# Summing rows from contiguous 8 MiB blocks instead of from 112 rows per partition

## Chip, cores, metric

One core of one Trainium2 chip. The time is device microseconds of that core, the median of several executions, all with a granted clock of 1.0. A profile is one execution, and its span is some 1.8 us shorter than the time measured for the same execution.

## The reference

```python
batch, seq, dim = 32, 512, 1024
x = np.random.randn(batch, seq, dim).astype(np.float32)      # 67.1 MB
out = (np.sum(x, axis=-1) * 0.5).astype(np.float32)          # 16384 sums, 64 KiB
```

16384 rows of 4 KiB are read, and each gives one number.

## The kernel before

The rows are cut into eight blocks of 128 partitions x 16 rows (8 MiB). Three buffers hold blocks; VectorE (DVE) sums them, ScalarE (ACT) takes half of the seventh and about half of the eighth. The first seven blocks come from one region in which partition p owns 112 rows in a row; block b takes rows 16b to 16b+15 of each partition. So a load is 128 runs of 64 KiB that lie 448 KiB apart, and the 112 results of a partition leave as one run of 448 B. The last block is a region of its own, 16 rows to a partition, loaded in five pieces so that little work is left after the last byte.

```python
own = rows - B                                   # 128 - 16 = 112
x_rows = x_flat[0 : P * own, :].rearrange("(p c) d -> p c d", p=P)
x_last = x_flat[P * own : N, :].rearrange("(p c) d -> p c d", p=P)
out_rows = out_flat[0 : P * own].rearrange("(p c) -> p c", p=P)
out_last = out_flat[P * own : N].rearrange("(p c) -> p c", p=P)
# ... cut ...
for b in range(n_blocks - 1):
    c0 = b * B
    t = x_pool.tile([P, B, D], fp32, name="xb")
    loads.append(nc.sync.dma_start(out=t, in_=x_rows[:, c0 : c0 + B, :]))
    h = B if b < n_blocks - 2 else B // 2
    nc.vector.reduce_sum(out=sums[:, c0 : c0 + h], in_=t[:, 0:h, :], axis=mybir.AxisListType.X)
    # ... res = sums * mul on DVE; rows h..B on ACT
# ... last block: five loads of x_last, then
early = nc.sync.dma_start(out=out_rows, in_=res[:, 0:own])
# ... sums of the last block on DVE and ACT
store = nc.sync.dma_start(out=out_last, in_=res[:, own:])
# ... the program ends when early and store have landed
```

## Time and profile before

| | before |
|---|---|
| time, median (6 runs) | 162.07 us (161.97 to 162.15) |
| span of the profile | 160.2 us |
| DMA engines busy | 97.4% |
| a block's landing to the next one's | 19.35 us (433.5 GB/s) |
| first block in use | 21.78 us |
| last load to end of span | 157.5 to 160.2 us |

The DMA engines are the bound. VectorE waits 1.9 us for every block after the first, and the reduce starts work as a clock for landings (the moments at which all bytes of a transfer have arrived): when a load is slow, the next start comes late and the idle time in its square brackets grows.

### The profile page before, as it was taken

The numbers are of one execution on the slowest core, as the hardware profiler recorded it, in microseconds if no ns is written. First come the engines' busy times: TensorE is split into PE (matmuls) and PEld (weight loads), VectorE is DVE, ScalarE is ACT, GpSimd is POOL, SyncE is SP. The second block draws the span as 40 slices with busy tenths as digits, with TensorE's granted clock in tenths as the row PEclk, the third lists the DMA queues.
The fourth block names the chain that finished last, engine by engine and source line by source line (L and its number), as shares of the span: only waits on it lengthen the run. The fifth ranks groups of instructions, "written<-read, shape, count | busy, mean of one in ns | idle before, by whom it ended". The sixth has DMA issues, their size and how long they took to land.

```text
span 160.2 us, 138 instructions
## 1 busy us (share of the span) xinstructions
DVE 119.3 (74%) x34; ACT 17.3 (11%) x31; POOL 0.2 (0%) x4
## 2 busy tenths in 40 slices
DVE  0000059997799969999599995999959999597443
ACT  0000000000000000000000000000000000599952
POOL 0000000000000000000000000000000000000000
DMA  7996996996996996997997998979969969999992
GB/s 278 507 524 262 524 524 262 524 524 262 524 524 262 524 524 262 524 475 311 524 442 344 524 409 376 524 311 475 524 278 507 524 278 507 393 393 425 430 399 72
DMA packets 2016, 67.18 MB, mean 419 GB/s; under 512 B 480, under 2 KB 608, under 8 KB 736
## 3 DMA queue, kind: packets, MB, share of 16 engines
q1 hardware_dynamic: 2016, 67.18, 97.4%
HBM read 67.11 MB, written 0.07 MB: 419 GB/s over the span
## 4 chain that ended last, share of the span: by engine, by line
DMA 75%; DVE 22%; SPq 1%; issue 0%; DVEq 0%
DMA xb<-in_x_dram 75%; DVE sums L96 22%; SPq L114 1%; DVE xb L80 0%; SPq L120 0%; SPq L94 0%; DVE res L99 0%; DVEq L205 0%
## 5 line engine op out<-in xcount | busy, mean ns | idle before, releaser
L96 DVE TENSOR_REDUCE sums<-xb 128x16 f32<-128x16384 f32 (+1 forms) x7 | 112.0, 16001 | 33.3 <-DMA xb<-in_x_dram 33.3
L70 ACT ACT_TABLE_LOAD x1 | 1.3, 1283 | 137.9 <-DMA xb<-in_x_dram 137.9
L70 ACT ACTIVATE xb<-xb 128x1024 f32<-128x1024 f32 x15 | 15.7, 1045 | 2.1 <-DMA xb<-in_x_dram 2.1
L80 DVE CUSTOM_DVE_ANT_0 xb<-xb 128x512 f32<-128x512 f32 (+1 forms) x9 | 5.6, 664 | 5.0 <-DMA xb<-in_x_dram 5.0
L70 ACT ACTIVATION_READ_ACCUMULATOR xb<-xb 128x1 f32 x15 | 2.8, 187 | 0.0
L99 DVE TENSOR_SCALAR res<-sums 128x16 f32<-128x16 f32 (+1 forms) x7 | 1.2, 174 | 0.2
L80 DVE DVE_READ_ACCUMULATOR2_ANT res<- 128x1 f32 x9 | 0.7, 83 | 0.0
L80 DVE CUSTOM_DVE_ANT_0 xb<-xb,part 128x224 f32<-128x224 f32 x1 | 0.5, 450 | 0.2 <-DMA xb<-in_x_dram 0.2
L191 POOL MEMSET const-bfloat16-1.0<- 128x1 bf16 x1 | 0.1, 101 | 0.0
L191 POOL MEMSET const-uint8-127<- 128x1 uint8 x1 | 0.1, 101 | 0.0
L191 POOL MEMSET const-float32-0.0<- 128x1 f32 x1 | 0.1, 98 | 0.2 <-issue 0.2
L191 POOL MEMSET const-float32-1.0<- 128x1 f32 x1 | 0.1, 98 | 0.0
L80 DVE DVE_READ_ACCUMULATOR2_ANT part<- 128x1 f32 x1 | 0.1, 83 | 0.0
## 6 DMA issues: line engine op xcount, KB each, us to landing
xb<-in_x_dram SPq DMA_DIRECT2D x1, 4096.0 KB, 31.1
xb<-in_x_dram SPq DMA_DIRECT2D x1, 2560.0 KB, 36.9
xb<-in_x_dram SPq DMA_DIRECT2D x1, 1024.0 KB, 38.9
xb<-in_x_dram SPq DMA_DIRECT2D x1, 288.0 KB, 39.1
xb<-in_x_dram SPq DMA_DIRECT2D x1, 224.0 KB, 39.2
xb<-in_x_dram SPq DMA_DIRECT2D x7, 40.8
out_dram<-res SPq DMA_DIRECT2D x1, 56.0 KB, 10.0
out_dram<-res SPq DMA_DIRECT2D x1, 8.0 KB, 1.4
```

The source lines that it names most:

```text
L70: acts.append(nc.scalar.activation(out=t[:, r, :], in_=t[:, r, :], func=mybir.ActivationFunctionType.Copy, scale=mul, accum_out=res[:, col ...
L80: return nc.vector.tensor_tensor_reduce(out=t[:, r, lo:mid], in0=t[:, r, lo:mid], in1=t[:, r, mid:hi], scale=mul, scalar=start, op0=ADD, o ...
L96: nc.vector.reduce_sum(out=sums[:, c0 : c0 + h], in_=t[:, 0:h, :], axis=mybir.AxisListType.X)
L99: nc.vector.tensor_single_scalar(out=res[:, c0 : c0 + h], in_=sums[:, c0 : c0 + h], scalar=mul, op=mybir.AluOpType.mult,)
L114: nc.sync.dma_start(out=t[:, lo:hi, :], in_=x_last[:, lo:hi, :])
L191: nc = _bacc.Bacc("TRN2", target_bir_lowering=False, num_devices=1)
```

## The change

The intent: each load reads 8 MiB in one piece. Partition p's run starts 64p KiB into the block, so the pitch from partition to partition is 64 KiB instead of 448. The price is that a partition's results of seven blocks are no longer neighbours in the output: the first store becomes 7 x 128 rows of 64 B.

```diff
-    x_rows = x_flat[0 : P * own, :].rearrange("(p c) d -> p c d", p=P)
-    x_last = x_flat[P * own : N, :].rearrange("(p c) d -> p c d", p=P)
-    out_rows = out_flat[0 : P * own].rearrange("(p c) -> p c", p=P)
-    out_last = out_flat[P * own : N].rearrange("(p c) -> p c", p=P)
+    x_blocks = x_flat.rearrange("(b p c) d -> b p c d", p=P, c=B)
+    out_blocks = out_flat.rearrange("(b p c) -> p b c", p=P, c=B)
 ...
-        loads.append(nc.sync.dma_start(out=t, in_=x_rows[:, c0 : c0 + B, :]))
+        loads.append(nc.sync.dma_start(out=t, in_=x_blocks[b]))
 ...  (last block: x_last[...] becomes x_blocks[n_blocks - 1, ...], the same addresses)
-    early = nc.sync.dma_start(out=out_rows, in_=res[:, 0:own])
+    early = nc.sync.dma_start(
+        out=out_blocks[:, 0 : n_blocks - 1, :],
+        in_=res[:, 0:own].rearrange("p (b c) -> p b c", c=B),
+    )
 ...
-    store = nc.sync.dma_start(out=out_last, in_=res[:, own:])
+    store = nc.sync.dma_start(out=out_blocks[:, n_blocks - 1, :], in_=res[:, own:])
```

More of the change, by code (lines that the diff above doesn't have):

```diff
@@ L114 @@
             nc.sync.dma_start(
-                out=t[:, lo:hi, :], in_=x_last[:, lo:hi, :]
+                out=t[:, lo:hi, :], in_=x_blocks[n_blocks - 1, :, lo:hi, :]
             )
@@ L120 @@
             nc.sync.dma_start(
-                out=t[:, B - 1, lo:hi], in_=x_last[:, B - 1, lo:hi]
+                out=t[:, B - 1, lo:hi], in_=x_blocks[n_blocks - 1, :, B - 1, lo:hi]
             )
         )
-    early = nc.sync.dma_start(out=out_rows, in_=res[:, 0:own])
+    early = nc.sync.dma_start(
+        out=out_blocks[:, 0 : n_blocks - 1, :],
+        in_=res[:, 0:own].rearrange("p (b c) -> p b c", c=B),
+    )
     on_act = {4, 5, 6, 7, 11, 12, 14}
```

## The prediction

> **What bounds the kernel now.** I read the page first: the busy shares, the DMA queue, the chain that ended last. Then the timeline of the reduce instructions, the DMA issues, and the busy time by window at the end of the span.
>
> ```profile
> DVE 119.3 (74%) x34; ACT 17.3 (11%) x31; POOL 0.2 (0%) x4
> ...
> q1 hardware_dynamic: 2016, 67.18, 97.4%
> ...
> DMA 75%; DVE 22%; SPq 1%; issue 0%; DVEq 0%
> ```
>
> VectorE is idle a quarter of the span, but the sixteen DMA engines hold a packet for 97.4% of it. The chain gives DVE 22%, and one could take that for a bottleneck. The list of the chain in order of time shows what these stretches are: two of the 17.23 us reduces, walked through because a load three blocks on reuses the buffer that the reduce frees.
>
> ```profile
> 21.78 17.22 DVE L96 TENSOR_REDUCE sums<-xb 128x16 f32<-128x16384 f32 x1 [21.78 <-DMA xb<-in_x_dram]
> ...
> 41.11 17.22 DVE L96 TENSOR_REDUCE sums<-xb 128x16 f32<-128x16384 f32 x1 [1.91 <-DMA xb<-in_x_dram]
> ...
> 60.46 17.22 DVE L96 TENSOR_REDUCE sums<-xb 128x16 f32<-128x16384 f32 x1 [1.91 <-DMA xb<-in_x_dram]
> ...
> 137.87 8.69 DVE L96 TENSOR_REDUCE sums<-xb 128x8 f32<-128x8192 f32 x1 [1.92 <-DMA xb<-in_x_dram]
> 147.58 0.69 DVE L80 CUSTOM_DVE_ANT_0 xb<-xb 128x512 f32<-128x512 f32 x1 [0.82 <-DMA xb<-in_x_dram]
> ...
> 153.68 0.69 DVE L80 CUSTOM_DVE_ANT_0 xb<-xb 128x512 f32<-128x512 f32 x1 [3.56 <-DMA xb<-in_x_dram]
> ```
>
> Every reduce waits 1.9 us for its data, so starts tell landings: one block every 19.35 us, from 21.78 to 137.87 in six steps of 116.09/6. A block is 128 x 16 x 4096 B = 8.389 MB, so 433.5 GB/s, without pause. When a reduce ends (39.0) and the load three blocks on is issued, one block is about to land (41.1) and another is still queued; the queue keeps some 21 us of work ahead. The freed buffer is therefore no bottleneck. The bound is the pace of the DMA engines on the loads.
>
> The end of the span, by window (us, DVE, ACT, POOL, clock, DMA share, GB/s), and the two stores:
>
> ```profile
> 153.68:157.55 3.87, 3.09 (x10) 3.34 (x6) 0.00 (x0) 1.00 0.84 330
> 157.55:158.60 1.05, 0.46 (x2) 0.00 (x0) 0.00 (x0) 1.00 0.00 0
> 158.60:159.44 0.84, 0.00 (x0) 0.00 (x0) 0.00 (x0) 1.00 0.11 10
> ...
> out_dram<-res SPq DMA_DIRECT2D x1, 56.0 KB, 10.0
> out_dram<-res SPq DMA_DIRECT2D x1, 8.0 KB, 1.4
> ```
>
> The big store is issued at 147.68, lands 10.0 us later at 157.7, behind the queued loads, just after the last load (157.47 in the chain). Then the DMA engines are empty until the 8 KB store, issued at 158.04 after the last sum. That one lands 1.4 us on, at 159.4; the span ends at 160.2.
>
> **What the Trainium skill says.** "DMA: Bandwidth & Descriptors", section "Where 436 GB/s comes from", puts a core's ceiling at 16 ports with 435.2 GB/s together. The trace agrees: 433.5 GB/s by blocks. In the DMA packet records each 64 KiB packet takes 2418 ns (median of 896), which over 16 engines is 433.6 GB/s. No layout can gain much on that.
>
> The same page, "Latency and other measured facts", row "HBM row pitch at large powers of two": copies of 128-partition tiles lose rate when the pitch from partition to partition is a large power of two, 512 KiB at 207 GB/s per direction, 2 MiB at 164, 4 MiB at 103. This is the one statement that makes the change look dangerous: before, the pitch is 112 rows x 4 KiB = 448 KiB, no power of two; after, it is 64 KiB, one. But it lies below the smallest pitch of that list, and the last block of the kernel before already has it (next part).
>
> The same page, "Why a DMA increments its semaphore by 16 and not by 1", paragraph "How many engines (k)": the slowest dimension of each side picks the number of engines, up to 16. The new store has three dimensions, 128 x 7 x 16 on both sides; the slowest is 128, so all 16 should share it. The built program confirms this shape; that 16 engines run it no run here shows yet.
>
> The same page, "Why small descriptors are slow (HBM only)": a fixed cost per packet weighs on small ones. The packet records of before agree: 64 B takes 11 ns (median), 448 B 25 ns, 8 KiB 309 ns, 64 KiB 2418 ns; that is some 8 ns plus 0.037 ns per byte.
>
> **The change, part by part.** The order of instructions on every engine is the same before and after, with the same waits; the build shows only new addresses and the store's shape. So there are two parts.
>
> *Loads.* Each of the seven big loads is still 128 runs of 64 KiB. The rows of a block now lie side by side: partition p starts at 64p KiB instead of 448p KiB. Nothing is longer, shorter or fewer, so only the rate at which memory answers could change. Its evidence is the last block, which in the kernel before already has this pitch, cut by rows. From the reduce timeline, its first piece (8 rows, 4.194 MB) takes 147.58 - 137.87 = 9.71 us, or 432 GB/s; its second (5 rows, 2.621 MB) takes 153.68 - 147.58 = 6.10 us, or 430 GB/s. The packets say it more closely: 1213 ns for 32 KiB fits the same line as 2418 ns for 64 KiB. A further argument, arithmetic of mine: 448 is 7 x 64, and 7p modulo 128 takes every value once, so modulo 8 MiB both layouts start their 128 partitions at the same set of addresses. A choice of memory channel by lower address bits would see the same mix. Loads: 0 us.
>
> Where addresses may still show is the start. In the packet records the first 16 packets begin at 1.0 to 1.9 us and take 2.4 to 3.3 us instead of 2.42; the excess is 7.4 us in sum, 0.46 us per engine. With other addresses this may be anything from 0 to about twice that: -0.5 to +0.5 us.
>
> *The big store.* It goes from 128 runs of 448 B to 896 runs of 64 B: from 8 packets per engine to 56. At the measured durations that is 8 x 25 ns = 0.20 us against 56 x 11 ns = 0.62 us, +0.42 us per engine. The old store's packets end at 157.18 in the records, so the new ones should end near 157.6 and land near 158.1. The last store's packets begin at 158.87. So 1.7 us of free DMA time takes up the 0.42 us, and the last wait of the program, for both stores, still ends with the 8 KB store at 159.4. On the path: 0 us; I allow 0.1 us for memory still busy with 896 partial writes.
>
> *Sum.* 21.78 (first block) + 116.09 (six more) + 19.68 (last block, to 157.55) + 0.49 (last sum, store issue at 158.04) + 1.4 (landing) + 0.76 (end) = 160.2 us of span. I leave every term, and add 0.05 for the store. The measured time lies about 1.9 us over the span: 162.06 becomes 162.1.
>
> **Rivals.** First, contiguous 8 MiB blocks could read faster, the evident intent. Against it stands the engine ceiling: 67.1 MB at 433.6 GB/s is 154.8 us by itself. The loads run from 1.0 to 157.0 us in the packet records, so at most about 1.2 us is to be had, the start and the small last pieces; the latter don't change. Best case 161.3 us, "same".
>
> Second, the power-of-two pitch could make the engines collide in memory. For: the skill's row, and all 16 engines would start in step within one 8 MiB region. Against: the last block's 432 and 430 GB/s. If the rate fell by 5%, 135 us of big loads would become 142 and the time 169; at the skill's 164 against 207, some 199. I hold this for unlikely.
>
> Third, the 64 B writes could take the place of the last wait. With 1.7 us free, 56 packets per engine must take more than (0.20 + 1.7) us / 56 = 34 ns each before anything is delayed; 11 ns is the figure for the same size in the last store, though over 8 packets only. At 60 ns the store takes 3.4 us and the last store slips by about 1.5 us: 163.5. For more than 2% it would take some 92 ns each. The same happens if the descriptors are made late; but they have the 10 us between issue and use.
>
> **Range and chances.** Runs of one kernel differ by 0.1 us here. The start gives half a microsecond either way, the store only upward. So 162.1 with 161.5 to 162.8. Faster by 2% needs 158.8, below what the ceiling allows: 0.01. Slower by 2% needs 165.3, so rival two, or three at eight times the measured packet time: 0.04. Within 2%: 0.95.
>
> **What would show it right or wrong.** Right: reduces start every 19.35 us; the first starts within half a microsecond of 21.78; big-load packets stay at 2418 ns; 896 store packets of some 11 ns end before 158; the chain still ends DMA load, last sum, 8 KB store. Wrong on loads: steps above 19.5 us with the reduces waiting longer than 1.9 us. Wrong on the store: its landing past 159.4, or the final wait named for it; DMA share in the window after 157.55 would be well over zero up to the last store.

## The result and the profile after

| | before | after |
|---|---|---|
| time, median of 6 | 162.07 us | 162.31 us |
| lowest to highest | 161.97 to 162.15 | 162.06 to 162.75 |
| ratio (95% interval) | | 1.002 (1.0005 to 1.0036) |
| span of the profiled run | 160.2 us | 161.0 us |

A ratio here is the mean time of one kernel's runs over that of the other's runs of the same rounds, so not quite the ratio of the medians quoted. The change is "same" by the 2% mark, but the interval leaves out 1: it is slower by some 0.2%, and it scatters more. The profiled run, at 162.75 us, is the slowest of its six, so its trace shows an ample dose of whatever costs.

Two lines of the page, kernel after:

```profile
q1 hardware_dynamic: 2784, 67.18, 97.8%
...
DMA 75%; DVE 22%; SPq 1%; issue 0%; DVEq 0%
```

Same bound, same chain; the packets rose from 2016 to 2784 by the 768 of the store. The reduces of the timeline, kernel after (start, duration, instruction, idle before it):

```profile
21.94 17.22 DVE L94 TENSOR_REDUCE sums<-xb 128x16 f32<-128x16384 f32 x1 [21.94 <-DMA xb<-in_x_dram]
...
79.98 17.22 DVE L94 TENSOR_REDUCE sums<-xb 128x16 f32<-128x16384 f32 x1 [1.92 <-DMA xb<-in_x_dram]
...
99.47 17.22 DVE L94 TENSOR_REDUCE sums<-xb 128x16 f32<-128x16384 f32 x1 [2.07 <-DMA xb<-in_x_dram]
...
118.94 17.22 DVE L94 TENSOR_REDUCE sums<-xb 128x16 f32<-128x16384 f32 x1 [2.04 <-DMA xb<-in_x_dram]
...
138.56 8.69 DVE L94 TENSOR_REDUCE sums<-xb 128x8 f32<-128x8192 f32 x1 [2.19 <-DMA xb<-in_x_dram]
```

Up to 79.98 the steps are the old ones; then they are 19.49, 19.47 and 19.62 us, and the idle time before the reduce grows with them. The loads themselves came late. The windows at the end, kernel after (us, DVE, ACT, POOL, clock, DMA share, GB/s), and its two stores:

```profile
157.55:158.60 1.05, 0.81 (x5) 0.49 (x2) 0.00 (x0) 1.00 0.54 59
158.60:159.44 0.84, 0.16 (x2) 0.00 (x0) 0.00 (x0) 1.00 0.00 0
...
out_dram<-res SPq DMA_DIRECT2D x1, 56.0 KB, 10.5
out_dram<-res SPq DMA_DIRECT2D x1, 8.0 KB, 1.4
```

The 64 B packets fill part of the first window (in the packet records they start between 157.40 and 158.17), then the DMA engines stand idle until the last store. That one is issued at 158.78 and lands 1.4 us later, as before. The big store, issued at 148.37, lands 10.5 us later, at 158.9, well before the last one's 160.2.

So the account of the 0.76 us between the two spans is: first block +0.16 (21.94 against 21.78), six steps +0.53 (116.62 against 116.09), last block +0.06 (19.74 against 19.68, to the last sum's start), end +0.01 (2.67 against 2.66). In the packet records the same shows one level down: after the first sixteen, 17 of the 64 KiB packets took over 2440 ns before (the median is 2418), and 184 after. They are called slow packets below. Most of those of the kernel after come in bursts: in order of start, six rounds of sixteen packets have 13 or more slow ones. The records do not name the engine.

### The profile page after: what moved, and what is told of

The parts are those of the page before. It is cut to its first block, busy times and chain, and to the rows that moved or that the text cites. A ratio compares the mean times of both kernels' runs of the same rounds, so it can differ in the third digit from the quotient of the medians.

```text
span 161.0 us, 138 instructions
## 1 busy us (share of the span) xinstructions
DVE 119.3 (74%) x34; ACT 17.3 (11%) x31; POOL 0.2 (0%) x4
## 2 busy tenths in 40 slices
DMA packets 2784, 67.18 MB, mean 417 GB/s; under 512 B 1248, under 2 KB 1376, under 8 KB 1504
## 3 DMA queue, kind: packets, MB, share of 16 engines
q1 hardware_dynamic: 2784, 67.18, 97.8%
## 4 chain that ended last, share of the span: by engine, by line
DMA 75%; DVE 22%; SPq 1%; issue 0%; DVEq 0%
DMA xb<-in_x_dram 75%; DVE sums L94 21%; SPq L112 1%; SPq L118 0%; DVE xb L78 0%; SPq L92 0%; DVE res L97 0%; DVEq L206 0%
## 6 DMA issues: line engine op xcount, KB each, us to landing
out_dram<-res SPq DMA_DIRECT2D x1, 56.0 KB, 10.5
```

## The experiments

Theories: **A**, the new load addresses cost; **B**, the 64 B store costs; **C**, chance of a chip or session. Twelve runs were made, in three sets, each on one chip and beside the kernel before. Kernels that put results at wrong places do so on purpose; work and waits are the same.

### The parts by themselves (first set)

**after_again**: the changed kernel, unedited.

> The changed kernel once more, for its own scatter and a second profile. Theory A (the loads' addresses cost: with 64 KiB pitch the engines read in step and now and then disturb each other): 162.2 to 162.4, scatter of some 0.5 us, ratio 1.001 to 1.003, and again load steps above 19.40 us in places, with some 64 KiB packets over 2440 ns in the middle of the stream. Theory B (the 64 B store costs): the same time, but load steps of 19.35 throughout. Theory C (chance of one chip or session): ratio within 0.0005 of 1.

Measured: 162.53 us (162.22 to 162.92, 6 runs) against 162.05 (11 runs), ratio 1.0027 (1.0015 to 1.0039). Its profile has 150 slow packets and steps up to 19.53 us, now from the third block to the fifth. C falls; where the bursts come differs from run to run.

**loads_only**: the new loads with the old store.

```diff
     early = nc.sync.dma_start(
-        out=out_blocks[:, 0 : n_blocks - 1, :],
-        in_=res[:, 0:own].rearrange("p (b c) -> p b c", c=B),
+        out=out_flat[0 : P * own].rearrange("(p c) -> p c", p=P),
+        in_=res[:, 0:own],
     )
```

> Contiguous loads of the changed kernel with the old store of 448 B rows (results land at wrong places on purpose). Theory A: as the changed kernel, 162.2 to 162.4. Theory B: as the kernel before, 162.05. Theory C: 162.05.

Measured: 162.50 us (162.35 to 162.72), ratio 1.0023 (1.001 to 1.0036); 93 slow packets. The whole cost is there without the new store; lines of its repeat stand with the third set.

**store_only**: the old loads with the new store.

```diff
-    early = nc.sync.dma_start(out=out_rows, in_=res[:, 0:own])
+    out_blocks = out_flat.rearrange("(b p c) -> p b c", p=P, c=B)
+    early = nc.sync.dma_start(
+        out=out_blocks[:, 0 : n_blocks - 1, :],
+        in_=res[:, 0:own].rearrange("p (b c) -> p b c", c=B),
+    )
```

> Loads of the kernel before with the new store of 64 B rows (wrong places on purpose). Theory A: 162.05 with a scatter of 0.2 us; 896 store packets of 11 ns, over some 0.4 us per engine, all before the last store. Theory B: 162.3.

Measured: 162.19 us (162.12 to 162.22), ratio 1.0006 (0.9994 to 1.0018): not told apart from before, though by time alone up to 0.18% is not excluded. 14 slow packets, steps of 19.35. Its windows:

```profile
156.80:157.80 1.00, 0.78 (x5) 0.73 (x2) 0.00 (x0) 1.00 0.85 140
157.80:159.00 1.20, 0.43 (x2) 0.00 (x0) 0.00 (x0) 1.00 0.00 0
159.00:159.40 0.40, 0.00 (x0) 0.00 (x0) 0.00 (x0) 1.00 0.23 21
```

The 896 store packets are over by 157.7; 1.2 us of idle DMA time follow, and only then comes the last store. The new store is hidden. Theory A (the addresses cost) holds, its reason (engines that disturb each other) is not tested; B falls.

**pitch512**: 128 rows to a partition, pitch 512 KiB instead of 448; right result, store rows of 448 B.

```diff
+    M = 8
+    x_groups = x_flat.rearrange("(g p h c) d -> g h p c d", p=P, h=M, c=B)
+    x_blocks = [x_groups[b // M, b % M] for b in range(n_blocks)]
+    out_groups = out_flat.rearrange("(g p k) -> p g k", p=P, k=M * B)
```

> 128 rows to a partition, so every block has a pitch of 512 KiB instead of 448 KiB; result correct, store of 448 B rows. Tells whether a power-of-two pitch is what matters. If the power of two as such costs (theory A in its address form): slower than before by 0.2 us or more, 162.3 to 163 or far above if the channels collide outright (a 5% loss of rate would be 169). If only contiguity or neighbourhood within 8 MiB matters: 162.05 as before. [...]

Measured: 162.73 us (162.60 to 162.81), ratio 1.004 (1.0028 to 1.0052), the slowest pitch of all. From its timeline:

```profile
22.32 17.22 DVE L96 TENSOR_REDUCE sums<-xb 128x16 f32<-128x16384 f32 x1 [22.32 <-DMA xb<-in_x_dram]
...
41.73 17.22 DVE L96 TENSOR_REDUCE sums<-xb 128x16 f32<-128x16384 f32 x1 [1.98 <-DMA xb<-in_x_dram]
...
61.21 17.22 DVE L96 TENSOR_REDUCE sums<-xb 128x16 f32<-128x16384 f32 x1 [2.05 <-DMA xb<-in_x_dram]
...
80.57 17.22 DVE L96 TENSOR_REDUCE sums<-xb 128x16 f32<-128x16384 f32 x1 [1.93 <-DMA xb<-in_x_dram]
```

Here the loss sits at the beginning: the first block is 0.5 us late, two steps are 19.41 and 19.48, then the pace is the old 19.35. The runs of this kernel lie far apart in memory, not side by side, and it is slower all the same; contiguity as such is not what costs.

### Other pitches (second set)

**before_again**: the kernel before, unedited.

> The kernel before, unchanged, run as if it were another: the floor of what this comparison can tell, and a second profile of it. Ratio within 0.0008 of 1; load steps 19.35 us throughout; fewer than 30 of the 64 KiB packets over 2440 ns after the first 16. If the profile shows bursts as the changed kernel's did (150 to 184 such packets), theory A (addresses) has no footing in the packets.

Measured: 162.07 us, ratio 1.0001 (0.9988 to 1.0015); 17 slow packets, as in its first profile. A difference of 0.1% is about what these rounds can tell.

**pitch320_192**, **pitch128**, **pitch256**: the stores of before; the loads from groups of m blocks, which gives a pitch of 64m KiB, with `G` = (5, 3), (2, 2, 2, 2) and (4, 4).

```diff
+    x_blocks, at = [], 0
+    for m in G:
+        g = x_flat[at : at + P * m * B, :].rearrange("(p h c) d -> h p c d", p=P, h=m, c=B)
+        x_blocks += [g[h] for h in range(m)]
+        at += P * m * B
 ...
-        loads.append(nc.sync.dma_start(out=t, in_=x_rows[:, c0 : c0 + B, :]))
+        loads.append(nc.sync.dma_start(out=t, in_=x_blocks[b]))
 ...  (the last block likewise)
```

> Stores of the kernel before; blocks 0 to 4 at a pitch of 320 KiB, blocks 5 to 7 at 192 KiB: neither a power of two (results at wrong places on purpose). If the power of two is what costs: 162.05 as before, steps 19.35. If any departure from the 448 KiB pitch costs, or smaller spans do: 162.3 to 162.7.

Measured: 162.20 us (162.04 to 162.37), ratio 1.0006 (0.9994 to 1.0019); steps of 19.35, 12 slow packets. Not told apart from before; by time alone this is no proof, since the interval reaches the 1.0019 that a 64 KiB pitch measured in the third set, and the packets carry the argument.

> Stores of the kernel before; every block at a pitch of 128 KiB (wrong places on purpose). Power of two costs: between 64 KiB (162.5) and 512 KiB (162.73), so 162.4 to 162.8, with bursts of slow packets. Otherwise 162.05.

Measured: 162.17 us (162.03 to 162.53), ratio 1.0009 (0.9997 to 1.0022); 28 slow packets. Less than expected, and not told apart from before.

> Stores of the kernel before; every block at a pitch of 256 KiB (wrong places on purpose). Power of two costs: 162.4 to 162.8, with bursts of slow packets. Otherwise 162.05.

Measured: 162.20 us (162.13 to 162.76), ratio 1.0014 (1.0 to 1.0028); 54 slow packets. Between. "Every power of two costs 0.3 us" fell in this set, unless the chip mattered, since 64 KiB had been measured on another one.

### 64 and 128 KiB on one chip, and narrower stores (third set)

**loads_only_2** and **pitch128_2**: the same kernels as loads_only and pitch128.

> The 64 KiB pitch with the old stores again, beside the 128 KiB pitch on one chip, since the two were measured on different chips. If 64 KiB itself costs (theory A): 162.3 to 162.6 again, with a burst somewhere in the middle and load steps over 19.40 us. If the cost belonged to that one chip: 162.05 to 162.2.

> The 128 KiB pitch with the old stores again. If the cost goes with the pitch and 128 KiB is nearly free of it: 162.1 to 162.25, below the 64 KiB kernel of the same rounds by 0.2 us. If chips make the difference: equal to it.

Measured: 162.42 us (162.07 to 162.62), ratio 1.0019 (1.0006 to 1.0031), 143 slow packets; and 162.38 us (162.10 to 162.53), ratio 1.0015 (1.0003 to 1.0028), 159 slow packets. From the timeline of loads_only_2:

```profile
41.37 17.22 DVE L94 TENSOR_REDUCE sums<-xb 128x16 f32<-128x16384 f32 x1 [1.89 <-DMA xb<-in_x_dram]
...
60.87 17.22 DVE L94 TENSOR_REDUCE sums<-xb 128x16 f32<-128x16384 f32 x1 [2.07 <-DMA xb<-in_x_dram]
...
80.31 17.22 DVE L94 TENSOR_REDUCE sums<-xb 128x16 f32<-128x16384 f32 x1 [2.01 <-DMA xb<-in_x_dram]
...
99.77 17.22 DVE L94 TENSOR_REDUCE sums<-xb 128x16 f32<-128x16384 f32 x1 [2.04 <-DMA xb<-in_x_dram]
```

Steps of 19.50, 19.44 and 19.46, with the old store. From the timeline of pitch128_2:

```profile
41.28 17.22 DVE L101 TENSOR_REDUCE sums<-xb 128x16 f32<-128x16384 f32 x1 [1.91 <-DMA xb<-in_x_dram]
...
60.69 17.22 DVE L101 TENSOR_REDUCE sums<-xb 128x16 f32<-128x16384 f32 x1 [1.98 <-DMA xb<-in_x_dram]
...
80.32 17.22 DVE L101 TENSOR_REDUCE sums<-xb 128x16 f32<-128x16384 f32 x1 [2.20 <-DMA xb<-in_x_dram]
```

Steps of 19.41 and 19.63: the same pattern. On this chip the two pitches do the same; my expectation that 128 KiB is nearly free of it was wrong. The cost of a power-of-two pitch varies from run to run and perhaps from chip to chip.

All profiles together, with the 64 KiB packets over 2440 ns after the first sixteen, how many of them began outside the stretch from 115 to 119 us, and the start of the first reduce:

| kernel (pitch of the first blocks, KiB) | slow packets | outside 115 to 119 us | first reduce, us |
|---|---|---|---|
| before, before_again, store_only, store_16B, store_4B (448) | 17, 17, 14, 13, 19 | 0, 0, 1, 0, 2 | 21.78, 21.84, 21.92, 21.87, 21.88 |
| pitch320_192 (320, then 192) | 12 | 0 | 21.86 |
| after, after_again, loads_only, loads_only_2 (64) | 184, 150, 93, 143 | 158, 134, 76, 124 | 21.94, 21.82, 22.18, 22.05 |
| pitch128, pitch128_2 (128) | 28, 159 | 13, 145 | 21.95, 21.95 |
| pitch256 (256) | 54 | 37 | 21.99 |
| pitch512 (512) | 43 | 33 | 22.32 |

All six profiles with a pitch that is no power of two have at most 19, all eight with one at least 28. The separation is wider than that: every profile has 10 to 26 slow packets between 115 and 119 us, about when the five small last loads are issued (before: 116.4 to 118.7), whatever the pitch. Outside that stretch it is 0 to 2 against 13 to 158.

**store_16B** and **store_4B**: the kernel before, with right results, its first store cut into pieces by a gap after each K sums in the result buffer (K = 4 and 1).

```diff
+    wide = res_pool.tile([P, own // K, 2 * K], fp32, name="wide")
 ...  (the sums of the first seven blocks go to wide[:, :, 0:K])
-    early = nc.sync.dma_start(out=out_rows, in_=res[:, 0:own])
+    early = nc.sync.dma_start(
+        out=out_rows.rearrange("p (a k) -> p a k", k=K), in_=wide[:, :, 0:K]
+    )
```

> The kernel before (same loads, right result) with its first store cut to 3584 pieces of 16 B, 224 per engine. The idle DMA time ahead of the last store is some 1.9 us. If packets follow each other at some 7 ns as the 64 B ones did in the changed kernel: 1.6 us, hidden, 162.05 to 162.25. If they cost 11 ns each: 2.5 us, +0.6 us, 162.7. If small writes stall memory (rival three), 164 and more.

> The same in 14336 pieces of 4 B, 896 per engine: more than the idle time can hold, so the cost must come out. At 7 ns a packet 6.3 us, less 1.9 us of room: +4.4 us, 166.5. At 11 ns: 9.9 us, +8 us, 170. If something else hides or bounds the store, no such step: 162 to 163.

Measured: 173.73 us, ratio 1.0732, and 242.25 us, ratio 1.498. By the cost of packets both expectations missed by far: +11.6 us where I had 0 to 0.6, +80 where I had 4 to 8. The first result falls under the branch left open for rival three, "164 and more". From the page of store_16B, then its windows, then its queue's waits:

```profile
out_dram<-wide SPq DMA_DIRECT2D x1, 56.0 KB, 23.3
out_dram<-res SPq DMA_DIRECT2D x1, 8.0 KB, 11.4
```

```profile
157.00:159.00 2.00, 0.55 (x4) 0.53 (x2) 0.00 (x0) 1.00 1.95 42
...
163.00:165.00 2.00, 0.00 (x0) 0.00 (x0) 0.00 (x0) 1.00 0.01 0
165.00:170.00 5.00, 0.00 (x0) 0.00 (x0) 0.00 (x0) 1.00 0.00 0
```

```profile
SPq L213 <- DMA out_dram<-wide: 10.8, 1, 10.8
```

The packets are sent by about 163 (their records have a median of 9 ns), and then the DMA records are as good as empty for seven microseconds; yet the store, issued at 147.76, lands only at 171.1, and the program waits 10.8 us for it. I read this so: a packet's record ends when the engine has sent it, the landing when memory has taken it; the trace shows the gap, not its reason. All sixteen engines are late, not one: the sixteen landing events of this store lie between 166.0 and 171.0 us. The Trainium skill, "DMA: Bandwidth & Descriptors", section "Anatomy of one DMA — SWDGE (gpsimd) path", says that the semaphore cannot fire until the last byte is confirmed landed. These stores go the other, hardware path, but the trace agrees: records over by about 163, landed at 171. From the first packet (156.85) to the landing, 3584 writes of 16 B took 14.2 us, 4.0 ns each over all engines. The small writes held up other work too: the last sum of store_16B waited 1.73 us for the last load instead of 0.15, and in store_4B the issue of the 8 KB store took 65.30 us instead of 0.34. The 4 B store landed 91.9 us after its issue at 147.79, so some 83 us for 14336 writes, 5.8 ns each. The 896 writes of 64 B in the changed kernel took at most 158.9 - 157.4 = 1.5 us with their landing, 1.6 ns each. Whether the cause is a size under 64 B, or that several pieces fall into the same 64 B of the output, these two kernels don't tell.

## Why the prediction was right

**The time.** 162.1 with 161.5 to 162.8 was forecast; 162.31 was measured, and 162.53 when repeated. That the range held is in part luck: it left 0.7 us upward for the start and the store and nothing for the pace of the loads, and most of what came, came from the pace. Single runs of the changed kernel reached 162.75 and, outside the range, 162.92.

**The bound and the ceiling**: right. The chain and the DMA share are unchanged, and no kernel with another pitch beat the one before; the first rival, faster reads, gave nothing.

**Loads, "0 us"**: the one term mis-sized. It measured about +0.3 us: 0.24 by the first medians, ratios 1.002 and 1.0027 for the whole change, 1.0023 and 1.0019 for the loads alone. By the prediction's own sign, a step above 19.5 us with a longer wait, the effect of the second rival (a power-of-two pitch slows the loads) did happen, at a fraction of a per cent and not at the 5% and more that I had set against it; that the engines collide in memory, its reason, is not shown. Two arguments failed. The last block of the kernel before was taken as proof that 64 KiB is harmless; but the trouble comes in bursts that spare many blocks (three of the six steps in the changed kernel's profile), and one block can miss them: in after_again and loads_only_2, with a 64 KiB pitch throughout, the 32 KiB packets of the last block are as quick as before (1213 ns at most), while in the changed kernel's first profile 10 of these 128 took over 1225 ns. And the arithmetic about equal sets of start addresses modulo 8 MiB was true but did not bear: 448 KiB and 64 KiB give the same set, and behave differently.

**The start, "-0.5 to +0.5 us"**: right in size; with a 64 KiB pitch the first block was in use 0.04 to 0.4 us later than the 21.78 of the first profile, while the profiles at 448 KiB reach from 21.78 to 21.92 by themselves.

**The big store, 0 us on the path**: right, and for the reason given: it ends in the idle time before the last store. Its 56 packets per engine follow each other at some 7 ns, so they took 0.4 us and not 0.62. Their records end at 158.18 and not "before 158", since the loads ran late (157.69 in store_only). That all sixteen engines share the store, which no run had shown when the prediction was made, this trace shows: sixteen landing events, 158.46 to 158.85. The allowance of 0.05 us cannot be told apart from the measurement (ratio 1.0006 with an interval that holds 1).

**Rival three** did not happen at 64 B, but a store of narrower pieces did become the last wait: at 16 B it costs 11.6 us. The median packet record, which the prediction used as the cost of a packet, does not show it (9 ns at 16 B and at 4 B). The mean does in part (28 ns at 16 B, some 140 at 4 B), and landing times show all of it.

**Two sums**, neither of which bears on the outcome: at 164 against 207 GB/s rival two comes to some 198 us, not 199 (135 us of loads become 170). And the best case of 161.3 has no working: 162.06 less the 1.2 us that it names is 160.9.

**Open**: why a power-of-two pitch brings bursts. That the engines start in step is not enough of a reason: in the changed kernel's profile the first sixteen packets start within 0.4 us, in loads_only_2 within 1.3 us, and both have bursts; in before_again they start within 0.5 us, and it has none. What in memory collides, and what the chip contributes, no run here settles; and besides 448 KiB only one kernel without a power of two was tried (320 and 192 KiB), once.

## What to carry to other kernels

When the DMA engines already move data at their ceiling in 64 KiB runs, putting the runs side by side gains nothing; what is left of the addresses is a small risk, and a power-of-two pitch was on its wrong side here, by 0.1 to 0.4%, at the lower end within the noise. A store of many 64 B rows was free here because it ended in idle DMA time before a later wait, but with pieces of 16 B and 4 B such a store became the end of the program; judge stores by their landing, not by how soon the packets are gone. And one undisturbed block is no proof for a stream: a cost that comes in bursts needs several blocks, several runs and the scatter beside the median.

## What the Trainium skill lacked or had wrong

- "DMA: Bandwidth & Descriptors", "Latency and other measured facts", row "HBM row pitch at large powers of two": its list for copies starts at 512 KiB (207 GB/s, where it calls 214 full), and says nothing of smaller pitches. For loads here, 512 KiB cost 0.4% (ratio 1.004) and 64 KiB 0.2% (1.0019 to 1.0027), with bursts of slow packets that vary from run to run.
- The same page, "Specifications", gives 512 B or more as the size for line rate, with a read-modify-write below. Between 448 B and 64 B nothing was lost on the path here (ratio 1.0006); between 64 B and 16 B the store's landing grew from 10.5 to 23.3 us after issue. The page names no step below 512 B; here one showed between 64 B and 16 B, whether by size or because several pieces share 64 B of the output.
- The same page, "Why small descriptors are slow (HBM only)": it counts a cost per packet and fixed descriptor bytes. The 16 B and 4 B packets have records of 9 ns in the median, but landed at 4.0 and 5.8 ns per write over all engines, that is 64 and 93 ns per engine; no page gives this.
